# Block sums of the second feed-forward network, made in DRAM: the pace at which a hybrid decoder kernel issues them is set anew

## The chip, the cores and the metric

The kernel runs on one core of one Trainium2 chip. The metric is the device time of one execution in microseconds; the time given for a kernel is the median over runs. Names of engines: PE is TensorE (matmuls; PEld its loading of weights), DVE is VectorE, ACT is ScalarE, POOL is GpSimd, SP is SyncE, which here only issues DMAs.

## What is computed

One layer of a decoder trunk on x of 512 rows by 1024 columns, all in fp32. With the sizes D_FF = 2816, 8 attention heads of 64, 8 indexer heads of 32, the 128 best keys of each query kept, and a recurrent branch of 1024 channels:

```python
x = x + 0.5 * swiglu(rmsnorm(x, ffn1_norm), ffn1_wg, ffn1_wu, ffn1_wd)
x = x + hybrid_mixer(rmsnorm(x, mix_norm), w_in, ...)
x = x + 0.5 * swiglu(rmsnorm(x, ffn2_norm), ffn2_wg, ffn2_wu, ffn2_wd)
return rmsnorm(x, final_norm)

def swiglu(x, w_gate, w_up, w_down):
    return (silu(x @ w_gate) * (x @ w_up)) @ w_down

def hybrid_mixer(h, w_in, ...):
    q, k, v, qi, ki, wi, xr, gr, ga_logit, gr_logit = split_columns(h @ w_in)
    att = dsa_attention(q, k, v, qi, ki, wi)   # index scores pick 128 keys a query
    rnn = rg_lru(causal_dwconv(xr), ...) * gelu(gr)
    merged = sigmoid(ga_logit) * (att @ w_att_proj) + sigmoid(gr_logit) * (rnn @ w_rnn_proj)
    return merged @ w_out
```

The gates of the recurrent branch (`rg_lru`) are products with 16 small blocks of weights, two of them to a tile of 128 channels.

## The kernel before

**Precision.** A matmul in fp32 is made of three in a faster format: each operand is split into a high part (`wh`, `yh`: a rounding copy on ACT) and a remainder (`wl`, `yl`: a subtraction on DVE), and high × high, low × high and high × low are added up in PSUM. Every weight tile thus goes the way DRAM → `wr` in SBUF (a DMA from SP's queue) → ACT's copy `wh` → DVE's remainder `wl` → PE.

**The stages.** First the first feed-forward network (up, gate, then down), then the mixer, then the second network. PE works through all of this in one fixed order. The up and down projections are computed by a block scheme with fewer products than the plain one (seven block products of half-size operands instead of eight). Its operands are sums of blocks: of activations (`cm`, partly added by DMAs on POOL's queue, line 161) and of weights.

**Block sums of weights in DRAM.** A part of the sums of weight blocks is not made when the tile is loaded, but ahead of time in DRAM: class `Blocks` (line 321 on) makes `s1` to `s4` of four blocks with eight moves, as listed by `stages()`: two base copies, then adds (accumulating DMAs, line 329) and copies that depend on each other. A move is a DMA of 256 KB (128 × 512 fp32). The tiles are called `scr`. Adds and copies are on POOL's queue. `sums_in_turn()` (line 339) interleaves several blocks, so that the stages of one block lie in successive groups. There are two lots of them:

- 2nd down projection: 10 blocks, 80 moves, in 15 groups. Here the base copies are issued by SP (line 1533), all others by POOL. In `run_jobs()`, at `k == 2` of job `i`, as many groups are issued as `len(sum_groups) * (i + 1) // SUMJOBS` asks for; from job `SUMS_FROM - 1` on, all that are left.
- 2nd up projection: 12 blocks, 96 moves, all on POOL. `sums_until(part)` (line 1085) issues moves until `part` of the 96 is out. It first does a "beat" if any is due: a `memset` of one column on DVE (line 1090) and a copy of it on POOL (line 1091), which holds POOL's queue back until DVE has come to this place; the moves themselves are at line 1094. From job `SUMS_FROM` on it is called with a part that grows to `SUMS_PART` in `SUMS_TIME` us of planned PE time; during the direct products of the up projection, six times, up to `SUMS_PART + DIRECT_PART`; the rest in the first `SUMS_STEPS` steps of its stream of block products.

The streamed `s` tiles of the 2nd up projection (sums that DVE and POOL make in SBUF: `s<-w2u` added by POOL's DMA, line 161, then `s<-s,wr` on DVE) follow in the same POOL queue.

**The mixer.** It is a list of 64 jobs, one weight tile each, in an order that is written out by hand (`ORDER`, line 51): `i`, `k`, `v`, `e`, `q`, `x`, `g`, `r`, `a` are tiles of the input projection, `R`, `A`, `O` those of the two branch projections and of the output projection. Counting from 0, job 35 is `a5`, 36 is `g7` and 37 is `r7`. For each job PE runs 24 matmuls, if the tile is full. At fixed places inside a job the next tiles are fetched on SP (`mixer_fetch`, line 1136; three `wr` buffers), copied by ACT (`mixer_begin`) and split by DVE (`mixer_prepare`). What follows a job (scaling, convolution, gates, index scores, attention) is written as generators in `follow` and `active`; `tick()` lets each go on when a planner (`class Plan`, line 62), which adds up estimated durations by engine, finds its inputs ready. So the order on each engine is settled when the program is built.

Two of these follow-ups matter here. `gate_weights(t)` (line 1282) loads the gate weights of recurrent tile `t`: a DMA on POOL's queue (`gr<-wrg`), ACT's copy `gw<-gr`, DVE's remainder. It is begun three jobs ahead of the job `x`t. `masks()` (line 1339) computes the index scores: PE's products `aux<-KI,QI` into PSUM banks of the kind `aux`, of which there are four, and ACT's `rl<-aux` which empties them. The index queries (`QI`) are put into place by a long run of small DMAs on SP.

At the mixer's end its output is written to `xrows` in DRAM by POOL (line 1552), and read from there into `rows(m, half)` by eight DMAs of 256 KB on SP (line 1893), at given steps of the second network.

Of the kernel before, what the change touches and what calls it, by code (L numbers as in the profile page):

```python
# [43 lines left out]
LEAD = 4  # L44
PLAIN1, PAIRS1, PLAIN2, PAIRS2, TAIL = 6, 8, 2, 10, 3
DIRECT1, DIRECT2 = 4, 4
SUMJOBS = 48
UNITS, SUMS_FROM, SUMS_PART, DIRECT_PART, SUMS_STEPS, SUMS_TIME = 6, 37, 0.8, 0.1, 44, 145


ORDER = """
# [127 lines left out]
def hybrid_kernel(ctx, tc, xt, vec, w1u, w1d, wm, wki, wrg, watt, wrnn, wout, w2u, w2d, gf, out):  # L179
# [4 lines left out]
    Q = plan.engine("SP", nc.sync)  # L184
# [1322 lines left out]
    def run_jobs():  # L1507
# [3 lines left out]
        for i, job in enumerate(jobs):  # L1511
# [6 lines left out]
            for k in range(n):  # L1518
# [10 lines left out]
                if k == 2:  # L1529
                    due_sums = len(sum_groups) * (i + 1) // SUMJOBS if i < SUMS_FROM - 1 else len(sum_groups)  # L1530
                    while sums_done[0] < min(due_sums, len(sum_groups)):
# [358 lines left out]
    d2 = block_down(hs, w2d, x, PLAIN2, PAIRS2, BLOCKS2D)  # L1890
    for m in range(NQ):
        for half in range(2):
            d2.tasks.setdefault(-96 + 10 * m + 5 * half, []).append(lambda m=m, half=half: Q.dma_start(
                rows(m, half), xrows[m * QB:(m + 1) * QB, half * S:(half + 1) * S]))
    steps, index, units, turned, tasks_at = d2.steps, d2.index, d2.units, d2.turned, d2.tasks_at
    banks = {}
# [30 lines left out]
    def rows(m, half):  # L1927
        return x[2 * m + half]
# [176 lines left out]
```

## Time and profile before

| | us |
|---|---|
| median of 3 runs | 1056.52 |
| lowest and highest of the 3 | 1056.05, 1057.02 |
| the profiled execution | 1056.97 |
| span of the profiled execution | 1055.2 |
| PE busy within the span | 1043.9 |
| DVE, ACT, POOL busy | 890.0, 664.9, 264.4 |

The span runs from the first to the last work on the core that the profiler records; 1.77 us of the execution lie outside it. Busy times count work only, not the issuing of DMAs by SP. In a row of the timeline stand the start and the duration in us, the engine, the line, the operation with its output and inputs, how many of them follow each other (x2), and in brackets how long the engine had been idle before, and what ended that. Nearly all compute rows have the line 173, and DMA rows the line 161, since helper objects record them; they are told apart by the names of their tiles. A window's row gives, for a stretch of the span, its length, the busy time and count of PE, PEld, DVE, ACT and POOL, the mean TensorE clock granted (1.00 is full speed), the busy share of the 16 DMA engines and the GB/s that they moved.

### The profile page before, as it was taken

Reading aid. Unit: us, or ns where it says so; the run is one execution under the profiler, and the core shown is the slowest. Engines: PE = TensorE matmul, PEld = TensorE weight load, DVE = VectorE, ACT = ScalarE, POOL = GpSimd, SP = SyncE. Lnnn points to the kernel's source line nnn. Section 1 sums busy time; section 2 is a strip of 40 time slices with the busy share of each in tenths; the row PEclk is TensorE's granted clock in tenths of the full one; section 3 lists DMA queues with packets and bytes.
Section 4 is the critical chain, followed back from the end, with each engine's and each line's share of the span. In section 5 each row is a group of like instructions: output and inputs, shape, how many; then the busy total and the mean of one; then the engine's idle time right before and its main releaser. Section 6 shows DMA issues by size and latency. Waiting matters only on the chain.

```text
span 1055.2 us, 16640 instructions
## 1 busy us (share of the span) xinstructions
PE 1043.9 (99%) x5672; PEld 898.4 (85%) x5672; DVE 890.0 (84%) x1770; ACT 664.9 (63%) x1250; POOL 264.4 (25%) x389
## 2 busy tenths in 40 slices
PE   9999999999999999999999999999999999999997
PEld 7889999989999787787888888888889888888885
DVE  6679999989968879899899966875889788899985
ACT  7456666656666657987776664444656666656864
POOL 0261323302431021222222444453732000000201
PEclk9999999999999999999999999999999999999999
DMA  9786999938963487777766888989994865556873
GB/s 328 168 168 171 259 234 225 236 92 242 255 153 102 137 225 203 180 188 225 190 189 177 209 189 190 269 228 308 263 276 101 229 218 193 183 164 215 230 211 125
DMA packets 99221, 214.97 MB, mean 204 GB/s; under 512 B 12416, under 2 KB 19456, under 8 KB 98432
## 3 DMA queue, kind: packets, MB, share of 16 engines
q1 hardware_dynamic: 62448, 139.26, 40.0%
q0 software_dynamic: 36256, 74.21, 36.1%
q8 instruction: 44, 0.72, 0.3%
q10 hardware_dynamic: 432, 0.44, 0.1%
q14 instruction: 41, 0.34, 0.1%
HBM read 202.06 MB, written 54.53 MB: 243 GB/s over the span
## 4 chain that ended last, share of the span: by engine, by line
PE 91%; DVE 3%; DMA 3%; ACT 2%; issue 1%; ACTq 0%; DVEq 0%
PE mm L173 64%; PE aux L173 27%; DMA s<-w2u 1%; DVE wl L173 1%; DMA cm<-cr 1%; DMA wr<-wout 1%; ACT wh L173 1%; DVE sg L173 0%; ACT r L173 0%; DVE ml L173 0%; ACT L173 0%; ACT mh L173 0%; ACT cm L173 0%; DVE am L173 0%; DVE s L173 0%
## 5 line engine op out<-in xcount | busy, mean ns | idle before, releaser
L173 DVE TENSOR_TENSOR wl<-wr,wh 128x1024 fp32r<-128x1024 f32 (+2 forms) x236 | 235.7, 1003 | 53.6 <-ACT wh L173 52.3
L173 ACT ACTIVATE wh<-wr 128x1024 fp32r<-128x1024 f32 (+2 forms) x237 | 206.4, 877 | 84.5 <-issue 20.8
L173 PE MATMUL mm<-cm,wh 128*128 128x256 f32 (+1 forms) x1184 | 241.2, 310 | 0.3 <-ACT tg L173 0.3
L173 PEld LDWEIGHTS mm<-cm,wh 128*128 128x128 f32 x1184 | 189.4, 191 | 7.9 <-ACT tg L173 0.5
L173 PE MATMUL mm<-cm,wl 128*128 128x256 f32 x736 | 172.7, 282 | 1.6 <-DVE wl L173 1.6
L173 PE MATMUL mm<-yh,wh 128*128 128x512 f32 (+1 forms) x416 | 164.8, 397 | 0.1
L173 PE MATMUL mm<-yl,wh 128*128 128x512 f32 (+1 forms) x416 | 162.3, 391 | 0.0
L173 PE MATMUL mm<-yh,wl 128*128 128x512 f32 x408 | 159.2, 390 | 0.0
L173 PEld LDWEIGHTS mm<-cm,wl 128*128 128x128 f32 x736 | 130.0, 190 | 8.2 <-DVE wl L173 2.0
L173 PE MATMUL aux<-cm,wh 128*128 128x512 f32 (+1 forms) x472 | 122.9, 379 | 0.0
L173 PEld LDWEIGHTS mm<-yh,wh 128*128 128x128 f32 (+1 forms) x416 | 78.2, 188 | 18.1 <-issue 1.7
L173 PEld LDWEIGHTS mm<-yl,wh 128*128 128x128 f32 (+1 forms) x416 | 77.6, 187 | 15.3 <-DVE yl L173 0.4
L173 PEld LDWEIGHTS mm<-yh,wl 128*128 128x128 f32 x408 | 76.6, 188 | 16.5
L173 ACT ACTIVATE wh<-s 128x512 fp32r<-128x512 f32 x96 | 58.7, 625 | 46.9 <-DVE s L173 37.6
L173 PEld LDWEIGHTS aux<-cm,wh 128*128 128x128 f32 x472 | 79.7, 189 | 9.4
L329 POOL DMA_DIRECT2D scr<-w2d x40 | 37.2, 1050 | 158.9 <-DMA scr<-w2d 135.6
L173 DVE TENSOR_TENSOR wl<-s,wh 128x512 fp32r<-128x512 f32 x96 | 65.4, 688 | 13.4 <-ACT wh L173 12.7
L173 PEld LDWEIGHTS aux<-cm,wl 128*128 128x128 f32 x440 | 68.8, 189 | 8.7
L173 PE MATMUL aux<-cm,wl 128*128 128x256 f32 x440 | 74.0, 281 | 0.0
L173 PE MATMUL mm<-wh,cm 128*128 128x512 f32 x240 | 73.9, 389 | 0.0
L161 POOL DMA_DIRECT2D s<-w1u x44 | 41.7, 1163 | 114.7 <-DVE wl L173 70.3
L161 POOL DMA_DIRECT2D cm<-h x18 | 15.5, 861 | 194.0 <-ACT cm L173 172.6
(267 smaller groups left out, 2126.5 us busy)
## 6 DMA issues: line engine op xcount, KB each, us to landing
wr<-scr SPq DMA_DIRECT2D x88, 256.0 KB, 3.0
wr<-wm SPq DMA_DIRECT2D x39, 512.0 KB, 4.2
scr<-w2u POOLq DMA_DIRECT2D x72, 256.0 KB, 6.3
s<-w1u POOLq DMA_DIRECT2D x44, 256.0 KB, 7.4
scr<-scr POOLq DMA_DIRECT2D x44, 256.0 KB, 6.1
scr<-w2d POOLq DMA_DIRECT2D x40, 256.0 KB, 6.3
wr<-w1u SPq DMA_DIRECT2D x19, 512.0 KB, 6.8
wr<-w1d SPq DMA_DIRECT2D x18, 512.0 KB, 4.2
```

Of the source, the lines that this page charges most:

```text
L161: return self.engine.dma_start(out, src, **kw)
L173: return call(*args, **kw)
L329: plain, adds = nc.gpsimd.dma_start, lambda o, i: nc.gpsimd.dma_start(o, i, accum_op=ALU.add)
```

## The change

Three lines. The groups of the 2nd down projection's sums are spread over 40 jobs instead of 48. The sums of the 2nd up projection begin with job 36 instead of 37 and go up to 92% of the moves instead of 80% in 148 us of planned time instead of 145; 5% instead of 10% are left for the direct products, and 3% instead of 10% for the stream. The eight loads of x rows stand at steps −80, −76, ... −52 relative to the start of the down projection instead of −96, −91, ... −61.

```diff
-SUMJOBS = 48
-UNITS, SUMS_FROM, SUMS_PART, DIRECT_PART, SUMS_STEPS, SUMS_TIME = 6, 37, 0.8, 0.1, 44, 145
+SUMJOBS = 40
+UNITS, SUMS_FROM, SUMS_PART, DIRECT_PART, SUMS_STEPS, SUMS_TIME = 6, 36, 0.92, 0.05, 44, 148
...
     d2 = block_down(hs, w2d, x, PLAIN2, PAIRS2, BLOCKS2D)
     for m in range(NQ):
         for half in range(2):
-            d2.tasks.setdefault(-96 + 10 * m + 5 * half, []).append(lambda m=m, half=half: Q.dma_start(
+            d2.tasks.setdefault(-80 + 8 * m + 4 * half, []).append(lambda m=m, half=half: Q.dma_start(
                 rows(m, half), xrows[m * QB:(m + 1) * QB, half * S:(half + 1) * S]))
```

The groups of the down projection's sums were issued at jobs 3, 6, 9, 12, 15, 19, 22, 25, 28, 31 and 35, and the last four at 36; now they are at 2, 5, 7, 10, 13, 15, 18, 21, 23, 26, 29, 31 and 34, and the last two at 35. Of the 96 moves of the up projection's sums, 77 were issued by the mixer's end, 10 during the direct products and 9 in the stream; now they are 89, 5 and 2. The order of the instructions on PE and on ACT is the same in both programs; DVE has five beats fewer, and so has POOL.

The first place is POOL in the first third of the mixer, before: `gr` are loads of gate weights (the 3rd and the 4th of eight), `scr_2775` to `scr_2777` belong to the first block of the down projection's sums, `scr_2779` and `scr_2781` to the second.

```order
L329 DMA scr_2775<-w2d 128x512
L329 DMA scr_2777<-w2d 128x512
L161 DMA gr_4728<-wrg 128x128
L161 DMA gr_4784<-wrg 128x128
L1533 DMA scr_2776<-scr_2775 16x4096
L329 DMA scr_2779<-w2d 128x512
L329 DMA scr_2781<-w2d 128x512
L329 DMA scr_2776<-w2d 128x512
```

The same place on POOL after:

```order
L329 DMA scr_2775<-w2d 128x512
L329 DMA scr_2777<-w2d 128x512
L161 DMA gr_4728<-wrg 128x128
L1533 DMA scr_2776<-scr_2775 16x4096
L329 DMA scr_2779<-w2d 128x512
L329 DMA scr_2781<-w2d 128x512
L161 DMA gr_4789<-wrg 128x128
L329 DMA scr_2776<-w2d 128x512
```

The 4th load of gate weights (`gr_4784` before, `gr_4789` after) has moved from ahead of the copy and the second block's two adds to behind them.

These two adds follow on base copies that SP issues. SP at the end of its run of loads into `QI`, before (`wr` are weight tiles of the mixer):

```order
L161 DMA QI_4333<-qil_4467 32x512
L161 DMA QI_4333<-qih_4466 32x512
L161 DMA QI_4333<-qil_4467 32x512
L161 DMA wr_4653<-wm 128x1024
L1533 DMA scr_2779<-w2d 128x512
L1533 DMA scr_2781<-w2d 128x512
L161 DMA wr_4704<-wm 128x1024
```

The same place on SP after:

```order
L161 DMA QI_4333<-qil_4469 32x512
L161 DMA QI_4333<-qih_4468 32x512
L161 DMA QI_4333<-qil_4469 32x512
L1533 DMA scr_2779<-w2d 128x512
L1533 DMA scr_2781<-w2d 128x512
L161 DMA wr_4657<-wm 128x1024
L161 DMA wr_4704<-wm 128x1024
```

The second block's base copies have moved ahead of one weight tile, and still stand behind the whole run of QI loads. The first block's base copies, which stood inside this run, now stand ahead of it.

The last place is POOL where the 2nd up projection's stream begins, before: `s` are streamed sums in SBUF, `cm` sums of activations, `scr` the sums in DRAM.

```order
L161 DMA s_1525_8198<-w2u 128x512
L161 DMA s_1526_8199<-w2u 128x512
L1091 COPY beat<-beat 128x1
L329 DMA scr_2834<-w2u 128x512
L1094 DMA scr_2842<-scr_2840 16x4096
L329 DMA scr_2848<-w2u 128x512
L161 DMA cm_8246<-ca_8216 128x256
L1091 COPY beat<-beat 128x1
L1094 DMA scr_2856<-scr_2855 16x4096
L161 DMA cm_8287<-ca_8264 128x256
```

The same place on POOL after:

```order
L161 DMA s_1525_8217<-w2u 128x512
L161 DMA s_1526_8218<-w2u 128x512
L1091 COPY beat<-beat 128x1
L329 DMA scr_2860<-w2u 128x512
L161 DMA cm_8263<-ca_8235 128x256
L161 DMA cm_8301<-ca_8281 128x256
L161 DMA cm_8345<-ca_8318 128x256
L1091 COPY beat<-beat 128x1
L329 DMA scr_2850<-w2u 128x512
L161 DMA cm_8390<-ca_8362 128x256
```

Between the streamed sums and the sums of activations there are now fewer moves of sums in DRAM.

## Prediction

> **What bounds the kernel now.** I read the page first: the span, then the busy time of each engine, then the two DMA queues.
>
> ```profile
> span 1055.2 us, 16640 instructions
> PE 1043.9 (99%) x5672; PEld 898.4 (85%) x5672; DVE 890.0 (84%) x1770; ACT 664.9 (63%) x1250; POOL 264.4 (25%) x389
> q0 software_dynamic: 36256, 74.21, 36.1%
> ```
>
> TensorE is busy for 1043.9 of 1055.2 us, and its order of matmuls is the same in both programs. So whatever the change gains must come out of the 11.3 us in which PE is not busy, and a stall that it adds to PE comes back as time, because PE has no slack later in which to make it good. Next the waits of PE: who ended them, for how long in all, how often, and the longest.
>
> ```profile
> PE mm L173 <- DVE wl L173: 1.6, 2, 0.9
> ```
>
> Then the timeline of PE around these two (start, duration, engine, line, operation, and in brackets the idle time and who ended it).
>
> ```profile
> 779.56 0.40 PE L173 MATMUL mm<-cm,wh 128*128 128x256 f32 x2
> 780.83 0.39 PE L173 MATMUL mm<-cm,wl 128*128 128x256 f32 x1 [0.87 <-DVE wl L173]
> 781.05 0.40 PE L173 MATMUL mm<-cm,wh 128*128 128x256 f32 x2
> 781.29 0.28 PE L173 MATMUL mm<-cm,wl 128*128 128x256 f32 x1
> ...
> 782.12 0.40 PE L173 MATMUL mm<-cm,wh 128*128 128x256 f32 x2
> 783.28 0.39 PE L173 MATMUL mm<-cm,wl 128*128 128x256 f32 x1 [0.77 <-DVE wl L173]
> ...
> 793.47 0.50 PE L173 MATMUL mm<-cm,wh 128*128 128x256 f32 x2 [0.26 <-ACT tg L173]
> ```
>
> Both are in the second up projection, just where its stream of block products begins. A pair of these matmuls takes 0.24 us (781.05 to 781.29), so the one at 780.83 was due at 779.80 and the one at 783.28 at 782.36: 1.03 and 0.92 us lost. With the 0.26 to 0.42 at 793.47 (by the bracket, and by spacing) that is **2.2 to 2.4 us, and all that the change can win back here**. Why DVE was late is in the rows of DVE and POOL.
>
> ```profile
> 779.48 0.69 DVE L173 TENSOR_TENSOR s<-s,wr 128x512 f32<-128x512 f32 x1 [2.91 <-DMA s<-w2u]
> 768.31 0.86 POOL L161 DMA_DIRECT2D s<-w2u  x1 [0.55 <-DMA cm<-cr]
> ```
>
> DVE waited 2.91 us for a transfer that POOL had issued at 768.31, 11.1 us before. It came late because its queue was full of block sums. The windows give the stretch (length, then busy time of PE, PEld, DVE, ACT and POOL with counts, granted clock, DMA share, GB/s): at 760 to 780 the 16 DMA engines are taken whole, and 20 us later they are not.
>
> ```profile
> 760.00:780.00 20.00, 19.95 (x143) 18.61 (x141) 15.29 (x32) 11.11 (x26) 10.63 (x15) 1.00 1.12 274
> 780.00:800.00 20.00, 18.15 (x125) 16.69 (x126) 19.47 (x42) 11.92 (x25) 5.55 (x10) 1.00 0.83 203
> ```
>
> **The 2nd up projection's sums (gain).** Of 96 moves, 89 instead of 77 are to be out when the mixer ends. In POOL's order the stretch between the first streamed `s` add and the one that came late holds 11 sum moves before and 5 after. A move takes queue time: q0 had 36.1% of 1055.2 us for 74.21 MB, 5.13 us per MB, or 1.35 us for 256 KB. Six fewer are 8.1 us less in front of a transfer that was 2.9 us late (POOL's own issue alone, at 0.55 us each, is 3.3). So this wait goes, and both PE stalls and the one at 793 with it: **−2.3 us** (−2.0 to −2.4). What is late next there, the list of PE's waits doesn't show: it has none in that stream behind 793.
>
> **The price of it in the mixer.** The rate of sums goes from 0.8 × 96 / 145 = 0.530 to 0.92 × 96 / 148 = 0.597 moves per us, 13% more, into a stretch that is full at its end:
>
> ```profile
> 660.00:680.00 20.00, 19.83 (x88) 16.11 (x87) 17.10 (x33) 9.22 (x14) 9.50 (x18) 1.00 1.04 293
> 667.91 1.06 ACT L173 ACTIVATE wh<-wr 128x1024 fp32r<-128x1024 f32 x1 [1.22 <-DMA wr<-wout]
> 672.00 0.39 PE L173 MATMUL mm<-mh,wh 128*128 128x512 f32 x1
> ```
>
> ACT already waits 1.22 us there for a weight tile, but PE multiplies with it only at 672.00, 3.0 us after ACT's 1.06 us are over. This lead is the cover: 13% on a wait of 1.2 us doesn't use it up. I take nothing, with 0.5 us as the other end. The x rows loaded later, and five beats fewer on DVE and POOL, touch nothing that waits: nothing.
>
> **The 2nd down projection's sums (the new stall).** Over 40 jobs instead of 48 the groups of moves come at other jobs, and this puts the 4th load of gate weights (`gr`) behind two accumulating adds on POOL instead of ahead of them (the piece of POOL's order shown above). Those adds wait for base copies that SP issues, and SP puts the pair behind its run of QI loads. The rows of before, of SP and then of POOL:
>
> ```profile
> 365.88 1.36 SPq L1533 DMA_DIRECT2D scr<-w2d  x2
> 367.29 0.60 SPq L161 DMA_DIRECT2D QI<-qil  x1
> ...
> 386.22 0.53 SPq L161 DMA_DIRECT2D wr<-wm  x1
> 386.79 1.15 SPq L1533 DMA_DIRECT2D scr<-w2d  x2
> ```
>
> ```profile
> 372.67 0.82 POOL L329 DMA_DIRECT2D scr<-w2d  x1 [2.13 <-DMA scr<-w2d]
> 373.22 1.40 POOL L161 DMA_DIRECT2D gr<-wrg  x2
> ```
>
> and some 18 us later
>
> ```profile
> 391.79 0.88 POOL L329 DMA_DIRECT2D scr<-w2d  x1 [15.48 <-DMA scr<-w2d]
> 393.45 1.67 POOL L329 DMA_DIRECT2D scr<-w2d  x2 [0.78 <-DMA scr<-w2d]
> ```
>
> Before, the load is the second of the two at 373.22, issued at about 373.8, long before its use. After, it comes behind the second pair's adds. SP issued that pair at 386.79. It now goes ahead of one `wr` load (0.57 us from 386.22 to 386.79), and the first pair has left the QI run (1.41 us from 365.88 to the next load at 367.29), because it goes out before the run starts: 386.79 − 0.57 − 1.41 = 384.8. From SP's issue to the first add took 391.79 − 386.79 = 5.0 us, to the second 6.7, and to what stands behind it 7.2 (an issue takes POOL 0.55 us, 372.67 to 373.22): the load is issued at **392.0**. SP's copies of this kind, and then the gate loads by the tile view of `gr`, land after:
>
> ```profile
> scr<-w2d SPq DMA_DIRECT2D x20, 256.0 KB, 4.2
> ```
>
> ```profile
> DMA to landing us min/median/max: 2.1/3.8/5.6
> ```
>
> With the median of 4.2 for the base copy instead of 5.0, and a second add right behind the first, the load would go out at 390.7, the early end. The weights land between 390.7 + 2.1 = 392.8 and 392.0 + 5.6 = 397.6. I take 4.4 us, between the median and the longest, because this load goes out directly behind two adds: 396.4. Who waits for it, on ACT and PE:
>
> ```profile
> 390.40 0.30 ACT L173 ACTIVATE gw<-gr 128x128 fp32r<-128x128 f32 x1
> 390.60 1.04 ACT L173 ACTIVATE wh<-wr 128x1024 fp32r<-128x1024 f32 x1
> 391.55 0.37 ACT L173 ACTIVATE rl<-aux 128x256 f32<-128x256 f32 x1
> ```
>
> ```profile
> 393.86 0.40 PE L173 MATMUL aux<-KI,QI 128*128 128x256 f32 x2
> 394.09 0.40 PE L173 MATMUL mm<-yh,wh 128*128 128x512 f32 x1
> ```
>
> ACT works in order, and nothing in its order changes. Its copy `gw` of this tile ran at 390.40, and queued behind it are `wh` and the `rl` that empties a bank of `aux`: `rl` ended 391.92, 1.52 us after `gw` began. There are four such banks, and the second of PE's two index matmuls at 393.86 (at 393.97) needs the bank that this `rl` empties. So with `gw` at 396.4 the bank comes free at 396.4 + 1.52 + 0.1 = 398.0, and PE stands from 393.97: **+4.0 us** (0.4 at the early end, 5.2 at the late one). Below nothing it can't be: nothing on PE becomes earlier here. No stall at all needs the load to land by 392.35. The four later gate loads also stand behind adds, three of them now a group later; but those adds' base copies have left SP a group, about three jobs, earlier, with no run of QI loads ahead of them. I price them at nothing; if one is late after all, it adds to case D.
>
> **The clock behind a stall.** The granted clock (seventh figure of a window) after the last matmul, which ended at 1047.6, and PE's first matmuls of the run:
>
> ```profile
> 1047.60:1050.00 2.40, 0.01 (x1) 0.00 (x0) 1.82 (x6) 1.90 (x5) 1.66 (x2) 1.00 0.30 113
> 1050.00:1052.00 2.00, 0.00 (x0) 0.00 (x0) 0.38 (x1) 0.35 (x1) 0.00 (x0) 0.51 0.74 277
> ```
>
> ```profile
> 1.04 3.79 PE L173 MATMUL aux<-mean 128*128 128x128 f32 x16 [1.04 <-DVE epst L173]
> ```
>
> and, the first in steps of 0.23 us,
>
> ```profile
> 6.18 0.39 PE L173 MATMUL mm<-yh,wh 128*128 128x512 f32 x1
> ```
>
> 2.4 us of idleness were enough for half clock here, while waits of 1 us at 780 left it at 1.00. So a stall of 4 us is likely to cut it. At the start of the run PE is at full rate only from 6.18, 5.1 us after its first matmul; half of that, 2.6 us, is the most that a cut costs, and if the cut comes late in the stall and little work meets it, 0.5. I take half of the most, as if the cut came when half of its spell is over: **+1.3 us**. [...]
>
> **Sum.** −2.3 + 4.0 + 1.3 = +3.0 us. The profiled execution took 1056.97 us, of which 1055.2 are span and 1.77 lie around it; it is 0.45 above the median of 1056.52. By the profile the span becomes 1058.2, and against the median the time is **1059.5**.
>
> **The rivals.**
>
> - A, the forecast: a stall of more than 2.4 us with a cut clock. 1056.52 − 2.4 + 2.4 + 0.5 = 1057.0 at the low end, 1056.52 − 2.0 + 5.2 + 2.6 = 1062.3 at the high end. Chance 0.50.
> - B, the stall without the cut, or a short one: for it speaks that waits of 1 us cost nothing more. 1056.52 − 2.3 + 4.0 = 1058.2; with the short end, 0.4, it is 1054.6. Chance 0.20. [...]
> - C, faster: the gate weights land by 392.35, and only the gain is left, 1056.52 − 2.3 = **1054.2** (1053.9 at the best). It decides at SP: the base pair would have to go out some 4 us earlier than I reckon, at 381, and for that the run of QI loads at 0.6 us each (0.60 at 367.29), which holds SP until 386.22, would have to begin earlier or move faster. The early end of my landing times comes within 0.5 us of it. Chance 0.18.
> - D, the change doesn't do at 780 what it says: the five moves left and the later x rows still make the `s` transfer late, or the denser mixer costs PE what is won. DMA share at 760 to 780 is 1.12, and taking 6 × 256 KB from a stretch that moves 274 GB/s × 20 us = 5.5 MB leaves 0.8 of it; that speaks against. 1059.5 + 2.3 = 1061.8. Chance 0.12.
>
> **How the numbers follow.** A is the likeliest: 1059.5. The range reaches from C's best, 1053.9, to A's late end, 1062.3; what is outside is the last of D and of A. About 0.2%, 2.1 us, is what a measurement of this kernel can tell from no change: faster is under 1054.4, slower over 1058.6. C is faster (0.18). B lies within but for a few longer stalls, and A's low end too: 0.28. The rest of A, and D, is slower: 0.54.
>
> **What would show it.** In the changed kernel's profile: `gr` issued by POOL at about 392, ACT waiting some 6 us for it ahead of `gw`, PE waiting for ACT's `rl` at about 394 for 4 us, and a granted clock below 1.00 in the window behind; from there all of PE's rows 4 to 5 us later; then at 780 no wait for `wl`, and DVE's wait for the `s` transfer gone. I am wrong if PE's rows at 400 stand where they stood (C), if the clock stays at 1.00 (B), or if `wl` still makes PE wait at the stream's start (D).

## The result, and the profile after

| | us |
|---|---|
| changed kernel, median of 6 runs | 1062.54 (1061.60 to 1067.19) |
| kernel before, median of 6 runs | 1056.77 (1056.05 to 1060.04) |
| ratio, with its 95% interval | 1.0051 (1.0036 to 1.0065) |
| changed kernel on another occasion, 5 runs | 1063.52 (1062.32 to 1064.29), ratio 1.0053 (1.0040 to 1.0067) |

The change makes the kernel slower, by 0.5%, 5.4 us on 1056.8. The first profile of it is of its longest run (1067.19, span 1065.4), the second, from the repeat, of its shortest (1062.32). I use both, because the difference between them is part of the answer.

The page's first lines and PE's waits (in all, times, longest), first profile:

```profile
span 1065.4 us, 16629 instructions
PE 1047.3 (98%) x5672; PEld 901.1 (85%) x5672; DVE 890.4 (84%) x1765; ACT 664.7 (62%) x1250; POOL 265.4 (25%) x384
```

```profile
PE aux L173 <- ACT rl L173: 7.1, 1, 7.1
PE mm L173 <- DVE wl L173: 0.6, 1, 0.6
```

The same waits in the second profile (the list has no wait for `wl`):

```profile
PE aux L173 <- ACT rl L173: 4.9, 1, 4.9
```

One new wait of PE stands in both, for ACT's `rl`, once, 7.1 or 4.9 us long. The waits for `wl`, 1.6 us before, are down to 0.6 or gone. The new one is at the place that was forecast. SP, POOL, ACT and PE around it, first profile (each row: start, duration, engine, line, operation, in brackets the idle time before it and who ended it):

```profile
386.57 1.27 SPq L161 DMA_DIRECT2D QI<-qil  x1
387.89 1.23 SPq L1533 DMA_DIRECT2D scr<-w2d  x2
389.21 1.01 SPq L161 DMA_DIRECT2D wr<-wm  x2
390.27 1.24 SPq L1533 DMA_DIRECT2D scr<-w2d  x2
391.62 1.28 SPq L161 DMA_DIRECT2D wr<-wm  x1
```

```profile
391.72 0.88 POOL L329 DMA_DIRECT2D scr<-w2d  x1 [20.31 <-DMA scr<-w2d]
393.67 0.83 POOL L329 DMA_DIRECT2D scr<-w2d  x1 [1.08 <-DMA scr<-w2d]
394.22 0.88 POOL L161 DMA_DIRECT2D gr<-wrg  x1
```

```profile
402.01 0.31 ACT L173 ACTIVATE gw<-gr 128x128 fp32r<-128x128 f32 x1 [9.14 <-DMA gr<-wrg]
402.23 1.04 ACT L173 ACTIVATE wh<-wr 128x1024 fp32r<-128x1024 f32 x1
403.18 0.36 ACT L173 ACTIVATE rl<-aux 128x256 f32<-128x256 f32 x1
```

```profile
396.23 0.28 PE L173 MATMUL aux<-KI,QI 128*128 128x256 f32 x1
403.59 0.58 PE L173 MATMUL aux<-KI,QI 128*128 128x256 f32 x1 [7.08 <-ACT rl L173]
403.97 0.63 PE L173 MATMUL mm<-yh,wh 128*128 128x512 f32 x1
404.40 0.63 PE L173 MATMUL mm<-yl,wh 128*128 128x512 f32 x1
```

Read it from the top: the second block's base copies leave SP only at 387.89, when the QI run is over; POOL, idle for 20.31 us until the first has landed, issues the two adds and then the gate load; the load lands 7.8 us after its issue, at 401.99, 0.3 us behind the second add, which took 8.0; ACT has waited 9.14 us for it, and the `rl` that PE needs comes two instructions behind. Between the last two rows of PE lie 0.43 us, and not 0.23: the clock is at half. The windows show how long (length, then busy time of PE, PEld, DVE, ACT, POOL, granted clock, DMA share, GB/s):

```profile
398.00:399.00 1.00, 0.00 (x0) 0.00 (x0) 0.00 (x0) 0.00 (x0) 0.00 (x0) 1.00 1.07 291
400.00:403.50 3.50, 0.00 (x0) 0.00 (x0) 1.11 (x4) 1.49 (x4) 1.63 (x4) 0.50 0.98 255
403.50:406.50 3.00, 2.91 (x7) 2.37 (x8) 2.79 (x6) 1.11 (x4) 2.55 (x4) 0.50 0.84 94
406.60:408.00 1.40, 1.40 (x8) 1.09 (x6) 0.69 (x2) 1.23 (x3) 0.38 (x1) 1.00 1.07 195
```

Of the low clock's stretch, PE had work in 3.0 us, which cost 1.5. In the second profile PE started again sooner, at 399.09, and the clock came back at about 405.2: 6.1 us of work at half speed, 3.0 us lost.

```profile
398.36:401.77 3.41, 2.68 (x7) 2.20 (x8) 3.27 (x6) 1.75 (x5) 3.04 (x5) 0.50 0.74 94
401.77:405.18 3.41, 3.41 (x11) 2.28 (x9) 2.52 (x5) 2.00 (x3) 0.51 (x1) 0.50 1.03 276
```

So the shorter stall paid the larger price behind it.

### The profile page after: what moved, and what is told of

Same layout as the page of the kernel before. It is cut to its first block, busy times and chain, and to the rows that moved or that the text cites. A ratio compares the mean times of both kernels' runs of the same rounds, so it can differ in the third digit from the quotient of the medians.

```text
span 1065.4 us, 16629 instructions
## 1 busy us (share of the span) xinstructions
PE 1047.3 (98%) x5672; PEld 901.1 (85%) x5672; DVE 890.4 (84%) x1765; ACT 664.7 (62%) x1250; POOL 265.4 (25%) x384
## 4 chain that ended last, share of the span: by engine, by line
PE 90%; DMA 3%; ACT 2%; DVE 2%; issue 1%; SPq 0%; ACTq 0%; DVEq 0%
PE mm L173 64%; PE aux L173 26%; DMA s<-w2u 2%; DMA wr<-wout 1%; DMA gr<-wrg 1%; DVE wl L173 1%; ACT wh L173 1%; ACT r L173 0%; DVE sg L173 0%; DMA wr<-w1u 0%; DVE ml L173 0%; ACT mh L173 0%; ACT L173 0%; ACT pm L173 0%; DVE s L173 0%
```

## The experiments

The theory was the forecast's: the 4th gate load, behind two adds on POOL that wait for base copies behind SP's QI run, holds ACT, ACT holds a bank of PSUM, PE stands, and the clock is cut. The first rival was that the denser sums load the DMA engines, wherever the gate load stands; the second, that the up projection's sums cost more at the mixer's end than they bring. Each kernel ran in rounds with the kernel before on the same chip, and ratios are to that. The kernel before itself had medians of 1057.3 to 1058.3 there.

**Two jobs' difference in pace.** From the changed kernel:

```diff
-SUMJOBS = 40
+SUMJOBS = 42
```

> The changed kernel, with the down projection's sums over 42 jobs instead of 40. That puts two gate loads, the 4th and the 6th, back ahead of the adds on POOL and moves three weight loads on SP; PE, ACT and DVE have the same order. Theory (the 4th gate load behind two adds holds ACT, ACT holds a bank, PE stands 5 to 7 us and the clock is cut): the stall and the low clock go, 1055 to 1056.5 us, that is 6 to 7 us under the changed kernel's 1062.5. Rival (the denser sums load the DMA engines in the mixer, wherever the gate load stands): 42 is hardly less dense than 40, so 1061 us or more.

Measured: 1054.50 us (1054.12 to 1056.07), ratio 0.9971 (0.9959 to 0.9982). The stall went, with nearly the same density of sums, so the first rival falls. The kernel is even faster than the kernel before, and half a microsecond under the range that I gave. PE's list has one wait left at this place:

```profile
PE aux L173 <- ACT rl L173: 0.5, 1, 0.5
```

```profile
390.90 0.30 ACT L173 ACTIVATE gw<-gr 128x128 fp32r<-128x128 f32 x1
393.71 1.06 ACT L173 ACTIVATE wh<-wr 128x1024 fp32r<-128x1024 f32 x1 [2.51 <-DMA wr<-wm]
```

The gate weights are in time here (`gw` at 390.90), but ACT now waits 2.51 us for the weight tile, which SP sends behind the second block's base copies. This is a smaller, second price of the new order: half a microsecond, which the forecast had not seen.

**One number in the kernel before.**

```diff
-SUMJOBS = 48
+SUMJOBS = 40
```

> The kernel before with one number changed: the down projection's sums over 40 jobs. Theory: the gate load's stall and the cut clock come alone, without the gain at 780: 1056.8 + 5.5 to 8.5, 1062.3 to 1065. Rival (the loss comes from the up projection's sums, begun sooner and denser at the mixer's end): 1056 to 1057.5.

Measured: 1066.34 us (1064.37 to 1067.54), ratio 1.0077 (1.0064 to 1.0091), 8 us more. The stall alone, then, without the gain: in its profile PE waits 6.2 us for `rl`. Five of its six runs, and the median, are above the range that I gave; the increase of 8 us lies within the 5.5 to 8.5 that I expected, but the kernel before was at 1058.33 on this occasion and not at 1056.8.

**The second line of numbers in the kernel before.**

```diff
-... = 6, 37, 0.8, 0.1, 44, 145
+... = 6, 36, 0.92, 0.05, 44, 148
```

> The kernel before with the second line of numbers changed alone (up projection's sums from job 36, to 92% in the mixer), the x rows where they were. Theory: no stall at the gate load, a wait of PE less at 780, 1 to 1.4 us off, and up to 0.3 us more waiting at 677 to 689: 1055.4 to 1056.2. Rival (the denser sums at the mixer's end cost more than they bring): 1057 to 1060.

Measured: 1054.45 us (1053.98 to 1054.51), ratio 0.9965 (0.9953 to 0.9977). The gain is larger than I expected after the first profile, and nothing is lost at the mixer's end: the second rival falls. POOL comes to the streamed sum that had come late (the fifth in its order) at 763.17 instead of 768.31, and DVE no longer waits for it (POOL and DVE of this kernel):

```profile
763.17 3.00 POOL L161 DMA_DIRECT2D s<-w2u  x3
```

```profile
776.66 0.69 DVE L173 TENSOR_TENSOR s<-s,wr 128x512 f32<-128x512 f32 x1
```

**The third line in the kernel before.** The steps of the eight x row loads alone:

```diff
-            d2.tasks.setdefault(-96 + 10 * m + 5 * half, [])...
+            d2.tasks.setdefault(-80 + 8 * m + 4 * half, [])...
```

> The kernel before with the third line alone: the eight loads of x rows later. Theory (the waits at 780 come from the sums in POOL's queue, which stay): the time of the kernel before within 1 us. Rival (the first x row's load, which SP issues at 780 into full DMA engines, is what makes the streamed sums late): 1.5 to 2.5 us less than before.

Measured: 1057.26 us (1054.68 to 1059.32), ratio 0.9998 (0.9987 to 1.0008): no difference. Its profile still has the two waits for `wl`:

```profile
PE mm L173 <- DVE wl L173: 1.9, 2, 1.1
```

**Which of the two orders holds the gate load: POOL's or SP's?** In the changed kernel the second block's base copies go out with the first block's, ahead of the QI run:

```diff
     sum_groups, sums_done = sums_in_turn(BLOCKS2D), [0]
+    sum_groups[0].extend(sum_groups[1][-2:])
+    del sum_groups[1][-2:]
```

> The changed kernel, but the base copies of the second block of the down projection's sums leave SP with those of the first block, ahead of the run of QI loads. On POOL the 4th gate load stays behind the second block's two adds. Theory (the adds hold the gate load up only because their base copies stand behind the QI run on SP): the adds go as soon as POOL comes to them, the gate load with them, some 15 us before its use; no stall, no low clock, and the first weight load behind the QI run goes out sooner than in the kernel with 42 jobs: 1054 to 1055.5 us. Rival (being behind two accumulating adds in POOL's queue is enough): the load still lands late, over 1059.

Measured: 1054.27 us (1054.10 to 1054.95), ratio 0.9968 (0.9955 to 0.9980). POOL's order is that of the changed kernel, with the gate load behind the adds, but the adds don't wait (POOL, then ACT):

```profile
369.72 1.77 POOL L329 DMA_DIRECT2D scr<-w2d  x2
370.83 1.26 POOL L161 DMA_DIRECT2D gr<-wrg  x1
```

```profile
390.73 0.30 ACT L173 ACTIVATE gw<-gr 128x128 fp32r<-128x128 f32 x1
```

So a place behind adds on POOL is not enough. It takes both: POOL's order, and base copies that stand behind 20 us of other loads on SP.

**Why did the load take 7 to 8 us to land?** In the changed kernel the third block's base copies go out with the first block's:

```diff
+    sum_groups[0].extend(sum_groups[2][-2:])
+    del sum_groups[2][-2:]
```

> The changed kernel, but the two base copies of the third block of the down projection's sums leave SP with those of the first block, ahead of the run of QI loads, instead of right behind those of the second block. The 4th gate load stays behind the second block's adds. It took 7.8 us to land in the changed kernel's profile, where 4.4 was forecast. Theory (what SP sends in one burst when the QI run is over, 2 MB of weights and base copies, holds the gate load up): half a MB less in the burst is about 2.7 us at the 5.13 us per MB that POOL's queue took over the span, halved where two queues share, so the load lands in 5 to 6.5 us, PE stands 3.5 to 6 us and the time is 1060 to 1061.5. Rival (only the two adds ahead of it in POOL's own queue make it late): landing 7 to 8 us, and 1062 to 1063.

Measured: 1061.49 us (1059.35 to 1063.97), ratio 1.0036 (1.0022 to 1.0049), by the ratios 1.6 to 1.8 us under the changed kernel, with intervals that overlap. In its profile, of the shortest of its seven runs, POOL issues the load at 390.08, it lands at 396.22, after 6.1 us instead of 7.2 and 7.8, and PE waits less:

```profile
396.24 0.31 ACT L173 ACTIVATE gw<-gr 128x128 fp32r<-128x128 f32 x1 [5.50 <-DMA gr<-wrg]
```

```profile
PE aux L173 <- ACT rl L173: 3.4, 1, 3.4
```

That fits the theory, but it is one profile, and the kernel above with the second block's base copies sent ahead speaks against it. There the gate load stood behind the same two adds while SP issued nothing but QI loads of 64 KB, and it took as long to land as with the burst; nobody waited, since it was needed only 12 us after that. (The 16 DMA engines were full there too: a share of 1.02 while it was under way, against 1.08 in the changed kernel's first profile.) Its landing (least, median and most of this one load):

```profile
DMA to landing us min/median/max: 7.7/7.7/7.7
```

So a burst of weights was not needed here for 7 to 8 us. What the load follows in each of these four profiles is the add just ahead of it in POOL's queue: it landed 0.2 us behind an add that took 6.5 us here, 0.2 and 0.3 behind adds of 7.6 and 8.0 in the changed kernel, and 0.4 behind one of 7.8 with the base copies sent ahead. Why an add takes 6.5 us in one place and 8.0 in another, and what part SP's burst has in that, no run here separates.

**The price of the low clock.** In the changed kernel, PE gets work in the place of the stall: 20 matmuls with a tile of zeros, into the open sum.

```diff
...
+                if n == 7:
...
+                    for _ in range(20):
+                        nc.tensor.matmul(opened[0], zeros[0], KI, start=False, stop=False)
                 pl = pls[qb, h] = aux()
```

> The changed kernel with 20 more matmuls of 512 columns on PE just ahead of the index matmul that waits for the bank. They multiply by a tile of zeros, so they add nothing to the open sum, and take 20 x 0.23 = 4.7 us of the stall. DVE makes the zeros, one subtraction of 128 columns more. Theory (the low clock behind the stall costs 1.5 to 2.5 us by itself): PE stands at most 3 us with the gate load as late as before, the clock is not cut, and the time is 1.5 to 2.5 us under that of the changed kernel. Rival (the low clock costs nothing, since after the stall the matmuls wait for other engines anyway): same time as the changed kernel.

Measured: 1062.46 us (1059.79 to 1063.13), ratio 1.0037 (1.0024 to 1.0050). This settled nothing by its time: four of nine runs were at 1059.8 to 1060.3 and five at 1062.5 to 1063.1. The mean granted clock of the span is 0.998 in all four of the shorter runs and 0.996 or 0.997 in four of the five longer ones (0.999 in the fifth), as if the clock was cut only in the longer ones; that was not shown. But its profile (a run of 1062.81) shows something that none of the theories had. PE, then the windows:

```profile
394.56 4.72 PE L1394 MATMUL mm<-KI,gw 128*128 128x512 f32 x20
401.16 0.39 PE L173 MATMUL aux<-KI,QI 128*128 128x256 f32 x1 [1.87 <-ACT rl L173]
```

```profile
401.10:401.90 0.80, 0.74 (x4) 0.65 (x5) 0.80 (x2) 0.80 (x4) 0.80 (x4) 1.00 0.84 84
402.10:405.30 3.20, 3.20 (x9) 2.60 (x8) 2.96 (x7) 1.78 (x4) 1.77 (x3) 0.50 1.10 225
```

PE had stood for only 1.87 us, and the clock was cut at 402.06, after PE had worked again for 0.9 us. So the fill was made longer, to leave no idle stretch:

```diff
-                    for _ in range(20):
+                    for _ in range(30):
```

> As the kernel with 20 zero matmuls ahead of the waiting index matmul, but with 30: 30 x 0.236 = 7.1 us of work in the place of the stall, which adds nothing to the open sum. 20 of them left 1.9 us of waiting in its profile, and the clock was cut all the same. Theory (the low clock costs about 2 us by itself, and PE without an idle stretch is spared it): at most 0.5 us of waiting is left, the clock stays at 1.00, and the time is that of the kernels without a stall, 1054.4, plus 7.1: 1061.5, that is 2 us under the changed kernel although PE does 7.1 us more. Rival (the low clock costs nothing): the time of the changed kernel or more, 1063.5 to 1065.

Measured: 1060.65 us (1060.48 to 1061.49), ratio 1.0036 (1.0023 to 1.0050). No wait is left, and the clock stays at full speed (PE and a window):

```profile
393.89 6.99 PE L1394 MATMUL mm<-KI,gw 128*128 128x512 f32 x30
400.72 0.28 PE L173 MATMUL aux<-KI,QI 128*128 128x256 f32 x1
```

```profile
401.00:402.00 1.00, 1.00 (x6) 0.78 (x6) 1.00 (x3) 0.24 (x1) 1.00 (x2) 1.00 0.63 88
```

With 7 us more of work PE is done sooner than the changed kernel: 1060.65 against 1062.54 and 1063.52. The medians are from different occasions and two chips, and the intervals of the ratios (1.0023 to 1.0050, and 1.0040 to 1.0067) overlap, so the times alone give 2 to 3 us only roughly. The matmul spacing in the profiles gives 1.5 to 3.0 for a cut. The rival, that the low clock costs nothing, asked for 1063.5 or more and falls.

**The changed kernel again**, for the second profile used above:

> The changed kernel itself once more, so that the other three kernels have its time on the same chip and a second profile shows how much the landing of the 4th gate load and the wait at the second up projection's stream differ between executions. Theory: the gate load lands in 6 to 8 us, PE stands 5 to 7 us, and where the first profile still had 0.8 us of waiting for wl at the stream's start this one may have none, as two kernels with the same sums there had; 1061 to 1064 us.

Measured: 1063.52 us, as in the table. The gate load landed in 7.2 us, PE stood for 4.9, just under the 5 to 7 expected, and there was no wait for `wl`.

**What in the second line of numbers brings the gain?** In the kernel before, no moves during the direct products, and more in the stream instead:

```diff
-... = 6, 37, 0.8, 0.1, 44, 145
+... = 6, 37, 0.8, 0.0, 44, 145
```

> The kernel before with one number changed: no moves of the up projection's sums during the direct products (a part of 0 instead of 0.1); 77 moves in the mixer as before, and 19 instead of 9 later, in the stream. Theory (the moves that POOL has to issue and wait for during the direct products are what makes the first streamed sums late): POOL issues the first streamed sums 4 to 5 us sooner, the waits for wl at 780 go, and the time is 1054.4 to 1055.5. Rival (it is the number of moves left at the mixer's end that counts, since the DMA engines get them in any case): the waits only move into the stream, 1056.5 to 1058.5.

Measured: 1053.98 us (1053.72 to 1054.41), ratio 0.9972 (0.9961 to 0.9983). The mixer has no move more than before, the stream has ten more, and the gain is whole; PE's list has only the waits at the start (1.0) and of 0.5 at 537. POOL issued the sum that had come late only 2.4 us sooner (765.93), and not 4 to 5, but it landed 7.0 us after its issue instead of 11.1. So it is the moves that POOL issues during the direct products, ahead of that streamed sum, that made it late; how many are left at the mixer's end doesn't matter here. This one number, the second line alone (1054.45), the changed kernel with the base copies sent ahead (1054.27) and the one with 42 jobs (1054.50) all beat both kernels; among each other they lie within 0.5 us, their ratios are 0.9965 to 0.9972 with overlapping intervals, and no run tells which is best.

## Why the prediction was right, and where it was off

The sign and the mechanism were right, and the size was too small: +3.0 us forecast, +5.4 measured by the ratio. The median of 1062.54 is 0.2 us above the late end of the stated range, 1062.3; by the ratio, 1056.52 × 1.0051 = 1061.9, it is within. The second profile's terms are −2.3 + 4.9 + 3.0 = +5.6 in place of −2.3 + 4.0 + 1.3. By its steps:

- **The gain, −2.3.** Shown: the second line of numbers alone takes the waits away (1054.45, 2.3 under the first median of before, and 3.7 by its ratio). The sum that had come late lands 10.9 us after its issue there, and landed 11.1 after it before: its queue was not the shorter by 8.1 us of moves, as my working said. POOL came to it 5.1 us sooner, and that covers the 2.9 us by which it was late. With no moves in the direct products its landing did become shorter, by 4 us. The number of moves was the right thing to look at; the price per move by queue time did not hold.
- **Nothing lost at the mixer's end, nothing by the x rows and the beats.** Right: no new wait of PE there in the kernel with the second line alone, and the x rows alone change nothing (0.9998).
- **The gate load issued at 392.0.** Right: 390.2 in the second profile and 394.2 in the first, whose PE was 2.4 us behind already from the start of the run. (The early end, 390.7, doesn't follow from its terms: 384.8 + 4.2, and 0.55 for each of two adds, is 390.1.)
- **Landing after 4.4 us.** This is the step that failed. It took 7.2 and 7.8 us, outside the 2.1 to 5.6 of before (second and first profile, issue and time to landing):

```profile
390.24 7.25 DMA gr<-wrg
394.22 7.78 DMA gr<-wrg
```

I had taken the eight gate loads of before as one kind, and they are two. Four went out with no add of POOL's queue under way and landed in 2.1 to 2.4 us; the other four went out behind one and took 5.2 to 5.6. My 4.4 lies between, where none landed. Two loads of each kind, before:

```profile
DMA to landing us min/median/max: 2.1/2.1/2.2
DMA to landing us min/median/max: 5.4/5.5/5.6
```

In the profile of the kernel before and the changed kernel's first, ten of the 16 gate loads went out behind an add that was under way. Every one landed after that add, by 0.15 to 0.72 us, and took 4.1 to 7.8; the six others took 2.1 to 2.4. So the load's price was, in these two profiles, the time that the add ahead still needed. POOL's 40 adds to these sums took 6.3 us in the median before, which, by estimate, puts the landing at 391.45 (the second add, 0.55 ahead of the load's 392.0) + 6.3 + 0.2 = 398.0 and the stall at 5.6 us; in the changed kernel the add took 7.6 and 8.0. What makes an add that slow stays open.

- **The stall, +4.0.** Measured 4.9 and 7.1. In the second profile the load went out 1.8 us sooner than forecast and took 2.8 longer to land; in the first, issue and PE were both some 2.3 us late and the landing took 3.4 longer. Both account for the wait to within 0.3 us.
- **The cut clock, +1.3.** It is cut, as forecast, and costs 1.5 to 3.0 by the rows; filling the stall takes it away; my term was too small. The clock was cut in the kernel with 20 zero matmuls too, where PE stood for only 1.87 us, and the low clock lasted 3.4 or 6.8 us in these profiles.
- **The rivals.** Case B falls (the clock was cut in each of the four profiles in which PE stood for 3.4 us or more: 3.4, 4.9, 6.2 and 7.1), C asked for the load by 392.35, and it was some 5 us later at the least. Of D, a rest of 0.6 us of waiting for `wl` stood in the first profile and not in the second; why the two differ is open. (C's best, 1053.9, doesn't follow from the terms either: 1056.52 − 2.4 is 1054.1.)

## What to carry to other kernels

When DMAs are spread anew over a queue, look for what else uses that queue in order, and follow each transfer from its issue to the bank or buffer that somebody waits for: 64 KB of gate weights cost 5 to 8 us here, through two engines that had work. POOL stood for 20.31 and 19.65 us here before an add whose base copy went through SP's queue, and the gate load waited behind it; so send such an input ahead of long runs on that other queue (1054.27), or put the urgent load in front (1054.50). And price a landing by the transfer that is under way just ahead of it in its own queue (ten gate loads landed 0.15 to 0.72 us behind theirs), not by the median of the same kind of load elsewhere (3.8 us, against 7.2 and 7.8).

## What was unexpected of the hardware

The clock was cut 2.4 to 4.6 us after the end of PE's last matmul in the profiles with a stall and at the end of the kernel before, but with 20 zero matmuls 2.8 us after it and when PE was at work again, after an idle stretch of 1.87 us. It stayed low for 3.4 us (third block's copies ahead, behind a stall of 3.4, and 20 zero matmuls, behind 1.9) or 6.8 us (both profiles of the changed kernel, behind 7.1 and 4.9, and the one with 40 jobs alone, behind 6.2). So the price of a stall was not in proportion to it here: PE lost 3.0 us behind a stall of 4.9, and 1.5 behind one of 7.1.

Four stretches of 3.41 us, the length of the shorter spell at low clock, show how busy PE was ahead of a change of the clock, or of none: the last 3.41 us ahead of the cut (20 zero matmuls); the stretch from 6.82 to 3.41 us ahead of the cut, and the first 3.41 us at low clock (both 40 jobs alone); and the last 3.41 us at low clock (the changed kernel's first profile; busy times of PE, PEld, DVE, ACT and POOL, granted clock, DMA share, GB/s):

```profile
398.65:402.06 3.41, 1.54 (x7) 0.98 (x6) 2.10 (x4) 2.48 (x6) 2.35 (x5) 1.00 0.69 141
392.34:395.75 3.41, 2.19 (x11) 1.54 (x9) 0.87 (x2) 0.00 (x0) 1.37 (x2) 1.00 1.07 337
399.16:402.57 3.41, 1.79 (x5) 1.50 (x6) 3.00 (x6) 2.59 (x6) 2.87 (x5) 0.50 0.68 130
403.17:406.58 3.41, 2.99 (x8) 2.41 (x9) 3.20 (x6) 1.44 (x5) 2.88 (x5) 0.50 0.79 93
```

PE was busy for 45% of the first, and the clock was cut at its end; for 64% of the second, and the clock was at full speed after it; for 52% of the third, and the clock stayed at half; for 88% of the fourth, and it came back to full speed. An idle stretch of 1.87 us lay ahead of a cut here, while the waits of 0.87 and 0.77 us at 780 in the kernel before left the clock at 1.00. What decides this was not shown.

The kernel before varies by 1054.8 to 1060.5 between runs, and the kernels that have neither the waits at 780 nor the stall only by 0.5 to 2 us; that these waits are what varies is likely, but was not shown.
